# Attention in steps of a large and a small query block, with whole chunks of filling between them

## The chip, the core and the metric

The kernel runs on one core of one Trainium2 chip. The metric is the device time of one launch in microseconds (us), as the median of several runs. The core has a matrix engine (TensorE, in the profile PE for the matmuls and PEld for its weight loads), VectorE (DVE), ScalarE (ACT), GpSimd (POOL) and SyncE (SP), which issues almost all DMAs. Matmul results lie in PSUM, which has eight banks of 128 partitions x 512 fp32 values; PE writes them, DVE and ACT read them out.

## What is computed

One layer of a streaming encoder: 1,024 frames of a new stream (prompt) and 32 next frames of a running one (sample), 1,024 channels, 16 heads of 64. The part that matters here is the attention of a head, causal, with a bias from cumulated forget gates:

```
s = jnp.einsum('bqhd,bkhd->bhqk', q.astype(jnp.float32), k.astype(jnp.float32))
bias = jnp.transpose(cq, (0, 2, 1))[:, :, :, None] - jnp.transpose(ck, (0, 2, 1))[:, :, None, :]
mask = qpos[:, None] >= kpos[None, :]
s = jnp.where(mask[None, None], s + bias, jnp.finfo(jnp.float32).min)
p = jax.nn.softmax(s, axis=-1)
o = jnp.einsum('bhqk,bkhd->bqhd', p, v.astype(jnp.float32))
```

A query block is 128 frames, so block i (0 to 7) of a head has 128 (i + 1) keys. Beside the attention stand ten projections of the normed input, a depthwise convolution of 31 taps with a LayerNorm, and three output projections.

## The kernel before

All projections are three matmuls per product (high and low parts of both operands, L104), in chunks of 352 columns: a chunk is 8 x 3 matmuls into one bank, and three chunks and one weight (load, cast on ACT L93, subtraction on POOL L96) make one of 8 tiles of a gate. The kernel has three parts: projections with the convolution's taps on DVE, the attention stage, and the output projections.

The attention stage is filled up: between its own work PE does the projections of the gates gb, ma and mb, whose results nobody needs until later. `filler()` hands out 22 tiles (66 chunks), `fill(n)` runs the next n eighths of a chunk (3 matmuls each), and ScalarE copies each finished chunk out (L755) for a store to DRAM. Also hidden in this stage are the last convolution channel's taps on DVE (L260) and the LayerNorm's sums (`layernorm()`, PE L993), advanced by `next(ln)`.

A block of a head goes through three calls:

- `scores()`: 2 matmuls (L917, L918) for up to 512 keys, else 2 x 2 in two banks; then on DVE the diagonal's mask (L920) and the row maximum (L922), on ACT the exp (L925), on DVE a reciprocal (L927), on POOL the division (L928). Blocks 0 to 3 are small (bank tag S1, one bank), 4 to 7 large (tag S, two banks). Each tag has one buffer, so a score waits until the exp before has read it.
- `turn()`: P is transposed on PE (L938), up to four 128x128 pieces per bank of the pool psT, and copied by ACT (first bank) and DVE (second bank) to the tile pt of its half of the head (L941).
- `values()`: once per half of a head (blocks 0 to 3 small, 4 to 7 large), when its four blocks are turned: pt times V (L952) in column tiles of 64, copied by ACT (L957) and added by DVE (L958).

Blocks follow in the order 4, 0, 5, 1, 6, 2, 7, 3, with scores four blocks ahead. The main loop does per block: scores of the block four ahead, turn of this one, `fill(4)` (12 matmuls), then, if the block before ended a half, its values. So the large half's values come behind block 3's turn and filling, the small half's a block later. Four samples of the running stream (`Sample`: 4 heads each, scores L861 and L862, turn L883 and L886, values L898) are put into the list after head 3, 7, 11 and 15's first block; their scores use the score banks of tag S.

PE's instructions stand in the order of the program; the orders of DVE, ACT, POOL and SP are a scheduler's.

PSUM in this stage: one bank pq and one pq2 in turn for the fillings, three for psS (S and S1), three for psT.

Of the kernel before, what the change touches and what calls it, by code (L numbers as in the profile page):

```python
# [8 lines left out]
F32 = mybir.dt.float32  # L9
# [7 lines left out]
T = 1024  # L17
TS = 32
TT = T + TS
PAST = 512  # L20
# [10 lines left out]
NFILL = 22  # L31
R_U, R_V, R_QK, R_G, R_A = 0.25, 0.17, 0.19, 0.27, 0.12
NWARM = 46
ORDER = (4, 0, 5, 1, 6, 2, 7, 3)
AHEAD = 4
SAT = (2, 6, 10, 14)
SKEYS = PAST + TS
VC = 260
# [12 lines left out]
def build(tc, xT, xt, wv, wf, ckT, cv, clT, stT, vec, cst, yT, kT, vO, lfO, cpT, csT):  # L51
    nc = tc.nc
    es = ExitStack()
    PS = bass.MemoryType.PSUM

    def pool(name, bufs=1, stack=es, **kw):
        return stack.enter_context(tc.tile_pool(name=name, bufs=bufs, reuse_waits="tile", **kw))
# [88 lines left out]
    def steps(key, rh, rl, pspool, evac):  # L146

        w = split.pop(key) if key in split else split_w(load_raw(key))
        for c in range(3):
            ps = pspool.tile([128, CH], F32, name="pj", tag="pj")  # L150
            for kt in range(KT):
                mms(ps, w, rh, rl, csl(c), range(kt, kt + 1), kt == 0, kt == KT - 1)
                beat()
                if (c, kt) == (0, 5) and not split:
                    fetch()
                if kt < KT - 1:
                    yield False
            with tc.high_priority(offset=4000):
                evac(c, csl(c), ps)
            yield True  # L160
# [13 lines left out]
    def t352(name, bufs):  # L174
        return sg.tile([128, CH], F32, name=name, tag=name, bufs=bufs)

    pq = pool("pq", 1, space=PS)
# [3 lines left out]
    class Banks:  # L181

        n = 0

        def tile(self, *a, **k):
            self.n += 1
            return (pq if self.n % 5 == 4 else pjA).tile(*a, **k)
# [172 lines left out]
    ks_t = cp.tile([128, 8, TS], F32, name="ks_t")  # L360
    os_t = cp.tile([128, 8, TS], F32, name="os_t")
    rs9 = cp.tile([128, 9], F32, name="rs9")
    cq = cp.tile([128, 4], F32, name="cq")
# [10 lines left out]
    rows = lambda t: min(128, TT - 128 * t)  # L374
# [138 lines left out]
    p2 = ExitStack()  # L513
# [49 lines left out]
    for c in range(4):  # L563
# [13 lines left out]
        for t in range(8):  # L577
            ps = pj.tile([128, 512], F32, name="pjv", tag="pj")
            n = 0
# [169 lines left out]
    def gate_steps(g, f, pj):  # L749
        def ev(c, sl, ps):  # L750
            t = t352("t", 3)
            if g == "ga":
                sides["silu"] = nc.scalar.activation(t, ps, AF.Silu)
            else:
                nc.scalar.copy(t, ps)  # L755
            nc.sync.dma_start(s_g[g][f, :, sl], t)

        return steps((g, f), X, XL, pj, ev)
# [30 lines left out]
    heads = [Head(h) for h in range(H)]  # L789
# [19 lines left out]
    cvt[0] = pool("cv7", 1, stack=p2, side="right")  # L809
    taps.extend(last + sums(7))  # L810
    psS = pool("psS", 1, stack=p2, space=PS)
    psT = pool("psT", 3, stack=p2, space=PS)
    pq2 = pool("pq2", 1, stack=p2, space=PS)

    class Banks2:

        n = 0

        def tile(self, *a, **k):
            self.n += 1  # L820
            return (pq, pq2)[self.n % 2].tile(*a, **k)

    pF = Banks2()
    ap = pool("ap", 2, stack=p2, side="right")

    fills = [("gb", f) for f in range(8)] + [(g, f) for g in ("ma", "mb") for f in range(8)]

    def filler():

        for n in range(NFILL):  # L830
            yield from gate_steps(*fills.pop(0), pF)

    flow = filler()

    def fill(n):
        for _ in range(n):
            next(flow, None)

    class Sample:
# [14 lines left out]

        def scores(self):
            g, kc, pf = self.g, self.kc, self.pf
            ps = psS.tile([128, 2, 512], F32, name="psS", tag="S")
            for j in range(4):
                rows = slice(64 * (j % 2), 64 * (j % 2) + 64)
                q = qs_t[rows, 2 * g + j // 2, :]  # L860
                nc.tensor.matmul(ps[32 * j:32 * j + 32, 0, :], q, kc[rows, j // 2, :], start=True, stop=True)  # L861
                nc.tensor.matmul(ps[32 * j:32 * j + 32, 1, :TS], q, ks_t[rows, 2 * g + j // 2, :],  # L862
                                 start=True, stop=True)
            nc.vector.scalar_tensor_tensor(pf[:, :PAST], ps[:, 0, :], cq[:, g:g + 1], pf[:, :PAST],
                                           op0=ALU.add, op1=ALU.subtract)
            nc.vector.scalar_tensor_tensor(pf[:, PAST:], ps[:, 1, :TS], cq[:, g:g + 1], pf[:, PAST:],
                                           op0=ALU.add, op1=ALU.subtract)
            nc.vector.tensor_add(pf[:, PAST:], pf[:, PAST:], smask)
            nm = ap.tile([128, 3], F32, name="nm", tag="nm", bufs=6)
            nc.vector.tensor_reduce(nm[:, 0:1], pf, axis=AX.X, op=ALU.max, negate=True)  # L870
            nc.scalar.activation(pf, pf, AF.Exp, bias=nm[:, 0:1], accum_out=nm[:, 1:2])
            nc.vector.reciprocal(nm[:, 2:3], nm[:, 1:2])
            nc.vector.tensor_scalar(pf, pf, nm[:, 2:3], None, op0=ALU.mult)
# [94 lines left out]
    for n, pt_ in enumerate(PT):  # L968
        for j in range(4 * n, 4 * n + 4, 2):
            nc.gpsimd.memset(pt_[:, j + 1, 128 * (j % 4):128 * (j % 4) + 128], 0.0)  # L970
    seq = []
    for h in heads:
        seq += [Block(h, i) for i in ORDER]
        if h.h - 1 in SAT:
            seq.insert(len(seq) - 7, Sample(SAT.index(h.h - 1)))

    def first(b):
        return getattr(b, "i", None) == ORDER[0]

    def start(b):  # L980
        if first(b):
            h = b.head
            if h.h % 2 == 0:
                h.ot = heads[h.h + 1].ot = ap.tile([128, T], F32, name="ot", tag="ot", bufs=2)
        b.scores()

    def pending(b):
        return isinstance(b, Sample) or b.i % 4 == 3

    def over_channels(acc, put):  # L990
        for c in range(3):
# [5 lines left out]
    def layernorm():  # L997

        shift = sides["shift"]
        for _ in range(4):  # L1000
            yield
        yield from over_channels(mean, lambda sl, ps: nc.scalar.mul(mean[:, sl], ps, 1.0 / D))

        def put(sl, ps):
            t = t352("t", 3)
            nc.scalar.activation(t, mean[:, sl], AF.Square)
            nc.vector.scalar_tensor_tensor(rstd[:, sl], ps, 1.0 / D, t, op0=ALU.mult, op1=ALU.subtract)  # L1007
            nc.vector.tensor_add(mean[:, sl], mean[:, sl], shift[:, sl])
            nc.vector.tensor_scalar(rstd[:, sl], rstd[:, sl], EPS, None, op0=ALU.add)

        yield from over_channels(rstd, put)
        for c in range(6):
            sl = slice(c * CH // 2, c * CH // 2 + CH // 2)
            v, y = rstd[:, sl], t352("t", 3)[:, :CH // 2]
            nc.scalar.activation(y, v, AF.Ln)
            nc.scalar.activation(y, y, AF.Exp, scale=-0.5)
            yield
            w = t352("t", 3)[:, :CH // 2]
            nc.vector.tensor_copy(w, v)
            newton(v, w, y)  # L1020
            yield
# [3 lines left out]
    ln = layernorm()  # L1025
    sides["shift"] = ap.tile([128, TT], F32, name="shift", bufs=1)
    nc.sync.dma_start(sides["shift"], s_m)
    start(seq[0])
    fill(8)
    for b in seq[1:AHEAD]:  # L1030
        start(b)
        fill(2)
    for n, b in enumerate(seq):
        if n + AHEAD < len(seq):
            start(seq[n + AHEAD])
        if n + AHEAD + 2 < len(seq) and first(seq[n + AHEAD + 2]):
            seq[n + AHEAD + 2].head.load()
        if n + AHEAD + 3 < len(seq) and isinstance(seq[n + AHEAD + 3], Sample):
            seq[n + AHEAD + 3].load()
        if isinstance(b, Sample):  # L1040
            fill(4)
            b.turn()
        else:
            b.turn()
            fill(4 if b.i > 2 or b.head.h != 8 else 0)
        if n >= 1 and pending(seq[n - 1]):
            seq[n - 1].values()
        if "ready" in sides:
            next(ln, None)
    seq[-1].values()  # L1050
    for _ in flow:
        pass
    p2.close()
# [8 lines left out]
    class Banks3:  # L1062
        n = 0
# [196 lines left out]
```

## Time and profile before

| | |
|---|---|
| median of 3 runs | 1400.67 us (1399.84 to 1401.39) |
| profiled execution | 1399.91 us, of which the span of instructions 1398.1 |
| PE busy | 1383.8 us (99%) |
| DVE, ACT, POOL busy | 866.8, 602.9, 624.7 us |
| attention stage | 601.1 to 1090.1 us of the span |

The profile is of one execution. In a timeline, a row has the start and the duration in us, then engine, line of the code, operation, output<-inputs, shape and how many equal instructions are merged; in brackets the idle time of the engine just before and what ended it. [...] A list of waits has, per engine and line, what was waited for, the total in us, the number and the longest.

### The profile page before, as it was taken

To read this page: it belongs to the slowest core of one execution; us is meant where nothing else is said; L and a number is where in the kernel's file an instruction comes from. 1 tells how busy PE (TensorE), PEld (TensorE's weight loads), DVE (VectorE), ACT (ScalarE), POOL (GpSimd) and SP (SyncE) were. 2 spreads that over 40 slices of the span, in tenths; PEclk is the share of its full clock that TensorE was granted. 3 is DMA by queue.
4 is the path that set the end of the run, shared out by engine and by line. 5 is a ranking of instruction groups with operands and counts; after the bars stand their busy time and mean duration, and the time that the engine had idled before them with its cause. 6 is when DMAs were issued, how large, how long until landed. Compare 5 with 4: busy or idle time off the path is not lost.

```text
span 1398.1 us, 23429 instructions
## 1 busy us (share of the span) xinstructions
PE 1383.8 (99%) x8999; PEld 1300.6 (93%) x8999; DVE 866.8 (62%) x1199; ACT 602.9 (43%) x1180; POOL 624.7 (45%) x541
## 2 busy tenths in 40 slices
PE   8999999999999999999999999999999999999999
PEld 7999999999999999998788888888888999999998
DVE  6687787888898998646656655644443497132111
ACT  6322334656464642245444545554554555222100
POOL 2324244657585875444443533332332366254320
PEclk9999999999999999999999999999999999999999
DMA  4243332424342375334545545454542778444431
GB/s 181 93 142 92 119 109 95 150 77 158 95 164 87 121 210 153 114 104 130 144 114 159 144 140 158 121 144 115 163 115 72 280 259 268 140 143 142 147 108 47
DMA packets 102288, 192.77 MB, mean 138 GB/s; under 512 B 17248, under 2 KB 70368, under 8 KB 102176
## 3 DMA queue, kind: packets, MB, share of 16 engines
q1 hardware_dynamic: 102032, 191.21, 44.4%
q8 instruction: 71, 1.16, 0.4%
q14 instruction: 41, 0.34, 0.1%
q10 hardware_dynamic: 144, 0.07, 0.0%
HBM read 125.58 MB, written 65.64 MB: 137 GB/s over the span
## 4 chain that ended last, share of the span: by engine, by line
PE 90%; DVE 3%; issue 3%; ACT 2%; DMA 1%; POOL 1%; SPq 0%; ACTq 0%; POOLq 0%; DVEq 0%
PE pj L104 66%; PE pjv L584 7%; PE po L952 5%; PE ptr L938 4%; PE psS L917 3%; PE psS L918 2%; POOL wl L96 1%; PE pst L700 1%; PE pst L699 1%; PE po L898 0%; DVE nm L922 0%; ACT P L925 0%; DVE y L1095 0%; PE ptx L429 0%; DMA xtok<-xt 0%
## 5 line engine op out<-in xcount | busy, mean ns | idle before, releaser
L104 PE MATMUL pj<-xh,wh 128*128 128x352 f32 (+2 forms) x1536 | 508.6, 331 | 0.1
L104 PE MATMUL pj<-xl,wh 128*128 128x352 f32 (+2 forms) x1536 | 494.7, 322 | 0.2 <-DVE xl L432 0.2
L104 PE MATMUL pj<-xh,wl 128*128 128x352 f32 (+2 forms) x1536 | 493.3, 321 | 0.6 <-POOL wl L96 0.6
L96 POOL TENSOR_TENSOR wl<-raw,wh 128x384 fp32r<-128x384 f32 (+1 forms) x258 | 320.8, 1271 | 277.3 <-ACT wh L93 238.5
L260 DVE SCALAR_TENSOR_TENSOR y<-u,vec_t,y 128x1086 f32<-128x1086 f32 x240 | 382.0, 1592 | 23.4 <-ACT y L257 19.3
L104 PEld LDWEIGHTS pj<-xh,wh 128*128 128x128 f32 x1536 | 288.6, 188 | 3.2 <-issue 1.2
L104 PEld LDWEIGHTS pj<-xh,wl 128*128 128x128 f32 x1536 | 289.3, 188 | 1.1 <-POOL wl L96 0.9
L104 PEld LDWEIGHTS pj<-xl,wh 128*128 128x128 f32 x1536 | 288.5, 188 | 1.4 <-DVE xl L432 1.2
L928 POOL TENSOR_SCALAR P<-P,nm 128x640 f32<-128x640 f32 (+7 forms) x128 | 117.4, 918 | 257.0 <-DVE nm L927 244.6
L93 ACT CAST wh<-raw 128x1024 fp32r<-128x1024 f32 x86 | 90.1, 1047 | 111.0 <-PE pj L104 80.3
L925 ACT ACTIVATE P<-psS,nm 128x640 f32<-128x640 f32 (+7 forms) x128 | 95.2, 744 | 58.1 <-DVE nm L922 54.3
L941 ACT COPY pt<-ptr 128x512 f32<-128x512 f32 (+3 forms) x128 | 64.7, 506 | 96.2 <-PE ptr L938 95.0
L922 DVE TENSOR_REDUCE nm<-psS 128x1 f32<-128x640 f32 (+7 forms) x128 | 96.5, 755 | 7.9 <-POOL P L928 0.5
L717 POOL TENSOR_TENSOR ql<-qn,qh 128x352 fp32r<-128x352 f32 (+1 forms) x48 | 65.4, 1363 | 68.4 <-ACT qh L716 55.0
L920 DVE TENSOR_TENSOR psS<-psS,cmask 128x128 f32<-128x128 f32 x128 | 38.0, 297 | 78.6 <-PE psS L918 78.1
L938 PE MATMUL ptr<-ident,P 128*128 128x128 f32 x576 | 84.6, 273 | 0.3 <-DVE rstd L1007 0.3
L952 PE MATMUL po<-pt,V 128*64 128x512 f32 (+1 forms) x384 | 75.6, 529 | 0.0
L938 PEld LDWEIGHTS ptr<-ident,P 128*128 128x128 f32 x576 | 68.5, 140 | 6.6 <-DVE rstd L1007 0.5
L584 PE MATMUL pjv<-vwh,xh 128*128 128x260 f32 x256 | 72.5, 283 | 0.0
L584 PE MATMUL pjv<-vwl,xh 128*128 128x260 f32 x256 | 72.4, 283 | 0.0
L584 PE MATMUL pjv<-vwh,xl 128*128 128x260 f32 x256 | 72.3, 282 | 0.0
L917 PE MATMUL psS<-KB,QB 128*128 128x384 f32 (+1 forms) x192 | 70.1, 366 | 2.0 <-ACT P L925 1.4
(200 smaller groups left out, 2239.8 us busy)
## 6 DMA issues: line engine op xcount, KB each, us to landing
raw<-wf SPq DMA_DIRECT2D x88, 512.0 KB
QB<-s_q SPq DMA_DIRECT2D x32, 256.0 KB
KB<-s_k SPq DMA_DIRECT2D x32, 256.0 KB
kT<-qn SPq DMA_DIRECT2D x8, 528.0 KB
s_ga<-t SPq DMA_DIRECT2D x24, 176.0 KB
s_gb<-t SPq DMA_DIRECT2D x24, 176.0 KB
s_ma<-t SPq DMA_DIRECT2D x24, 176.0 KB
s_mb<-t SPq DMA_DIRECT2D x24, 176.0 KB
```

What stands on the lines that cost most here:

```text
L93: nc.scalar.copy(wh, raw)
L96: nc.gpsimd.tensor_sub(wl[:, k0:k1, :], raw[:, k0:k1, :], f32(wh[:, k0:k1, :]))
L104: nc.tensor.matmul(ps, a[:, kt, :], b(kt, sl), start=(first and n == 0), stop=(last and n == N - 1))
L260: t = nc.vector.scalar_tensor_tensor(y, u[:, i:i + CW], w, y, op0=ALU.mult, op1=ALU.add)
L584: nc.tensor.matmul(ps[:, :VC], a, b, start=(n == 0), stop=(n == 23))
L717: nc.gpsimd.tensor_sub(ql[:, :n], qn[:, o], f32(qh[:, :n]))
L917: nc.tensor.matmul(ps[:, b, :w], QB[:, qsl], KB[:, ksl], start=True, stop=False)
L922: nc.vector.tensor_reduce(nm[:, 0:1], ps[:, :nb, :w], axis=AX.XY, op=ALU.max, negate=True)
L925: nc.scalar.activation(P[:, :nk].rearrange("p (b w) -> p b w", b=nb), ps[:, :nb, :w], AF.Exp, bias=nm[:, 0:1], accum_out=nm[:, 1:2])
L928: nc.gpsimd.tensor_scalar(P[:, :nk], P[:, :nk], nm[:, 2:3], 1.0, op0=ALU.mult, op1=ALU.mult)
L938: nc.tensor.transpose(pt[:, 128 * j:128 * j + 128], P[:, 128 * (4 * u + j):128 * (4 * u + j) + 128], ident)
L952: nc.tensor.matmul(po[64 * o:64 * o + 64, q0:], V[:, j + o, hd], p[:, j + o, q0:], start=(j == 0), stop=(j == njb - 2), skip_group_check=True)
```

## The change

The list of blocks becomes a list of 64 steps, each with a large block (4 + j) and a small one (j) of the same head. A step does the scores of both blocks of the step two ahead, at a head's start (every fourth step) the two values of the head before, one behind the other, then both turns, and then `fill(8)`, one whole chunk. Fillings have one bank (pq), psT has four; the samples' scores use two banks of psT, and their three calls stand in consecutive steps. Loads of heads stand three steps ahead of a head's first turn, those of samples three steps ahead of their scores. `next(ln)` runs twice per step. One chunk of filling is left for the end, behind the last values.

```diff
-ORDER = (4, 0, 5, 1, 6, 2, 7, 3)
-AHEAD = 4
...
-    psT = pool("psT", 3, stack=p2, space=PS)
-    pq2 = pool("pq2", 1, stack=p2, space=PS)
...
+    psT = pool("psT", 4, stack=p2, space=PS)
...
-            yield from gate_steps(*fills.pop(0), pF)
+            yield from gate_steps(*fills.pop(0), pq)
...
-            ps = psS.tile([128, 2, 512], F32, name="psS", tag="S")
+            ps = [psT.tile([128, 512], F32, name="psR", tag="T") for _ in range(2)]
...
+    seq = [(Block(h, 4 + j), Block(h, j)) for h in heads for j in range(4)]
...
+    sample = {4 * h + 5: Sample(g) for g, h in enumerate(SAT)}
...
-    start(seq[0])
+    start(0)
     fill(8)
-    for b in seq[1:AHEAD]:
-        start(b)
-        fill(2)
-    for n, b in enumerate(seq):
-        if n + AHEAD < len(seq):
-            start(seq[n + AHEAD])
...
-            fill(4 if b.i > 2 or b.head.h != 8 else 0)
-        if n >= 1 and pending(seq[n - 1]):
-            seq[n - 1].values()
+    start(1)
+    heads[1].load()
+    for k in range(NS):
+        start(k + 2)
+        if k + 5 < NS and k % 4 == 3:
+            seq[k + 5][0].head.load()
+        if k + 3 in sample:
+            sample[k + 3].load()
+        if k % 4 == 0 and k:
+            for b in seq[k - 1]:
+                b.values()
+        if k - 2 in sample:
+            sample[k - 2].values()
+        if k in sample:
+            sample[k].scores()
+        for b in seq[k]:
             b.turn()
+        if k - 1 in sample:
+            sample[k - 1].turn()
+        fill(8)
         if "ready" in sides:
             next(ln, None)
-    seq[-1].values()
+            next(ln, None)
+    for b in seq[-1]:
+        b.values()
```

What the built programs have on PE at the end of the first head, before: the values of its large half stand alone between a filling and the next scores (po is the values' bank, psS the scores', ptr2 the turns', pj the fillings').

```order
L104 MATMUL pj_6793<-xl_87,wh_6653 128x352
L952 MATMUL po_6829<-pt2_6440,V_6121 64x512 x6
L952 MATMUL po_6829<-pt2_6440,V_6121 64x256 x2
L917 MATMUL psS_6840<-KB_6623,QB_6621 128x448
L918 MATMUL psS_6840<-KA_6622,QA_6620 128x448
L917 MATMUL psS_6840<-KB_6623,QB_6621 128x448
L918 MATMUL psS_6840<-KA_6622,QA_6620 128x448
L938 MATMUL ptr2_6852<-ident_189,P_6701 128x128 x4
```

The small half's values follow 12 filling matmuls later. The same place on PE after, from the small block's scores on:

```order
L904 MATMUL psS_6832<-KB_6525,QB_6523 128x384
L905 MATMUL psS_6832<-KA_6524,QA_6522 128x384
L939 MATMUL po_6842<-pt2_6437,V_6121 64x512 x6
L939 MATMUL po_6842<-pt2_6437,V_6121 64x256 x2
L939 MATMUL po_6853<-pt1_6436,V_6121 64x512 x2
L939 MATMUL po_6853<-pt1_6436,V_6121 64x256 x2
L925 MATMUL ptr2_6860<-ident_189,P_6670 128x128 x4
L925 MATMUL ptr2_6866<-ident_189,P_6670 128x128
L925 MATMUL ptr2_6869<-ident_189,P_6680 128x128
L102 MATMUL pj_6872<-xh_86,wh_6702 128x352
```

Both halves' values now stand together, between scores and turns, and three turning banks are asked for right behind them.

The start of the stage on PE, before: ahead of the scores of block 6 (448 columns per bank) stand those of block 1 and six filling matmuls.

```order
L917 MATMUL psS_6529<-KB_6112,QB_6110 128x256
L918 MATMUL psS_6529<-KA_6111,QA_6109 128x256
L104 MATMUL pj_6503<-xh_86,wh_6343 128x352
L104 MATMUL pj_6503<-xh_86,wl_6345 128x352
L104 MATMUL pj_6503<-xl_87,wh_6343 128x352
L104 MATMUL pj_6503<-xh_86,wh_6343 128x352
L104 MATMUL pj_6503<-xh_86,wl_6345 128x352
L104 MATMUL pj_6503<-xl_87,wh_6343 128x352
L917 MATMUL psS_6545<-KB_6112,QB_6110 128x448
```

After, from the scores of block 5 on:

```order
L904 MATMUL psS_6500<-KB_6112,QB_6110 128x384
L905 MATMUL psS_6500<-KA_6111,QA_6109 128x384
L904 MATMUL psS_6500<-KB_6112,QB_6110 128x384
L905 MATMUL psS_6500<-KA_6111,QA_6109 128x384
L904 MATMUL psS_6512<-KB_6112,QB_6110 128x256
L905 MATMUL psS_6512<-KA_6111,QA_6109 128x256
L904 MATMUL psS_6534<-KB_6112,QB_6110 128x448
```

No filling is left between the scores of blocks 5 and 6, which use the same two banks.

DVE at the first sample's scores (pf is the sample's row tile), before: the sample's scores are read in two operations (the rows of pf), and the reads of a block's scores lie before and after.

```order
L920 TENSOR_TENSOR psS_7314<-psS_7314,cmask_191 128x128
L941 COPY pt2_6440<-ptr2_7332 128x3x128
L922 TENSOR_REDUCE nm_7320<-psS_7314 128x1
L927 RECIPROCAL nm_7320<-nm_7320 128x1
L864 SCALAR_TENSOR_TENSOR pf_7256<-psS_7361,cq_198,pf_7256 128x512
L866 SCALAR_TENSOR_TENSOR pf_7256<-psS_7361,cq_198,pf_7256 128x32
```

After, DVE in the first sample's step:

```order
L907 TENSOR_TENSOR psS_7530<-psS_7530,cmask_191 128x128
L909 TENSOR_REDUCE nm_7536<-psS_7530 128x1
L907 TENSOR_TENSOR psS_7542<-psS_7542,cmask_191 128x128
L851 SCALAR_TENSOR_TENSOR pf_7308<-psR_7552,cq_198,pf_7308 128x512
L853 SCALAR_TENSOR_TENSOR pf_7308<-psR_7553,cq_198,pf_7308 128x32
L909 TENSOR_REDUCE nm_7546<-psS_7542 128x1
```

The sample's scores are now read behind the large block's mask and reduction and the small block's mask, and from two banks of psT.

More of the change, by code (lines that the diff above doesn't have):

```diff
@@ L811, in build @@
     psS = pool("psS", 1, stack=p2, space=PS)
-    psT = pool("psT", 3, stack=p2, space=PS)
-    pq2 = pool("pq2", 1, stack=p2, space=PS)
[L815 to L823, printed above, removed]
+    psT = pool("psT", 4, stack=p2, space=PS)
     ap = pool("ap", 2, stack=p2, side="right")
@@ L860, in scores @@
                 q = qs_t[rows, 2 * g + j // 2, :]
-                nc.tensor.matmul(ps[32 * j:32 * j + 32, 0, :], q, kc[rows, j // 2, :], start=True, stop=True)
-                nc.tensor.matmul(ps[32 * j:32 * j + 32, 1, :TS], q, ks_t[rows, 2 * g + j // 2, :],
+                nc.tensor.matmul(ps[0][32 * j:32 * j + 32, :], q, kc[rows, j // 2, :], start=True, stop=True)
+                nc.tensor.matmul(ps[1][32 * j:32 * j + 32, :TS], q, ks_t[rows, 2 * g + j // 2, :],
                                  start=True, stop=True)
-            nc.vector.scalar_tensor_tensor(pf[:, :PAST], ps[:, 0, :], cq[:, g:g + 1], pf[:, :PAST],
+            nc.vector.scalar_tensor_tensor(pf[:, :PAST], ps[0], cq[:, g:g + 1], pf[:, :PAST],
                                            op0=ALU.add, op1=ALU.subtract)
-            nc.vector.scalar_tensor_tensor(pf[:, PAST:], ps[:, 1, :TS], cq[:, g:g + 1], pf[:, PAST:],
+            nc.vector.scalar_tensor_tensor(pf[:, PAST:], ps[1][:, :TS], cq[:, g:g + 1], pf[:, PAST:],
                                            op0=ALU.add, op1=ALU.subtract)
@@ L970, in build, with start @@
             nc.gpsimd.memset(pt_[:, j + 1, 128 * (j % 4):128 * (j % 4) + 128], 0.0)
[L971 to L983, printed above, removed]
+    seq = [(Block(h, 4 + j), Block(h, j)) for h in heads for j in range(4)]
+    NS = len(seq)
+    def start(k):
+        if k < NS:
+            h = seq[k][0].head
+            if k % 8 == 0:
                 h.ot = heads[h.h + 1].ot = ap.tile([128, T], F32, name="ot", tag="ot", bufs=2)
-        b.scores()
-    def pending(b):
-        return isinstance(b, Sample) or b.i % 4 == 3
+            for b in seq[k]:
+                b.scores()
+    sample = {4 * h + 5: Sample(g) for g, h in enumerate(SAT)}
     def over_channels(acc, put):
@@ L1027, in build @@
     nc.sync.dma_start(sides["shift"], s_m)
-    start(seq[0])
+    start(0)
     fill(8)
-    for b in seq[1:AHEAD]:
-        start(b)
-        fill(2)
-    for n, b in enumerate(seq):
-        if n + AHEAD < len(seq):
-            start(seq[n + AHEAD])
[L1036 to L1041, printed above, removed]
-            b.turn()
-        else:
-            b.turn()
-            fill(4 if b.i > 2 or b.head.h != 8 else 0)
-        if n >= 1 and pending(seq[n - 1]):
-            seq[n - 1].values()
+    start(1)
[13 more added lines that the diff above has]
+            sample[k].scores()
+        for b in seq[k]:
+            b.turn()
+        if k - 1 in sample:
+            sample[k - 1].turn()
+        fill(8)
         if "ready" in sides:
             next(ln, None)
-    seq[-1].values()
+            next(ln, None)
+    for b in seq[-1]:
+        b.values()
     for _ in flow:
```

## The prediction

> **What bounds the kernel now.** I read the page first: which engine is full, and over what.
>
> ```profile
> PE 1383.8 (99%) x8999; PEld 1300.6 (93%) x8999; DVE 866.8 (62%) x1199; ACT 602.9 (43%) x1180; POOL 624.7 (45%) x541
> ```
>
> TensorE (PE) is full. The change touches only the attention stage, so next I asked for the busy times of that stage alone (from 601.1 us, the first scores, to 1090.1, the last values) and for PE's waits in it.
>
> ```profile
> 601.10:1090.10 489.00, 484.39 (x3187) 413.00 (x3185) 268.55 (x588) 244.53 (x540) 181.72 (x196) 1.00 0.46 129
> ```
>
> ```profile
> PE psS L861 <- ACT P L925: 2.3, 2, 1.3
> PE psS L917 <- ACT P L925: 1.4, 1, 1.4
> PE psS L917 <- ACT t L753: 0.6, 1, 0.6
> PE ptr L938 <- DVE rstd L1007: 0.3, 1, 0.3
> ```
>
> The columns of the first are the stretch, its length, then PE, PEld, DVE, ACT, POOL busy, clock, DMA share, GB/s. PE lacks 4.6 us of 489, and the four rows of waits (total, times, longest) name all of it: two of the four sample scores, one score at the start, the first score (banks of the old pools), one turn behind the LayerNorm. The granted clock is 1.00. So no more than 4.6 us can come from waits; anything else must come from PE's own time, and a busy PE here is not PE at its peak. That shows only in the starts of neighbouring matmuls. First PE's timeline at a head's end:
>
> ```profile
> 1025.45 0.32 PE L104 MATMUL pj<-xl,wh 128*128 128x352 f32 x1
> 1025.71 3.23 PE L952 MATMUL po<-pt,V 128*64 128x512 f32 x16
> 1028.87 0.47 PE L917 MATMUL psS<-KB,QB 128*128 128x448 f32 x1
> 1029.18 0.37 PE L918 MATMUL psS<-KA,QA 68*128 68x448 f32 x1
> 1029.39 0.37 PE L917 MATMUL psS<-KB,QB 128*128 128x448 f32 x1
> ...
> 1029.80 0.71 PE L938 MATMUL ptr<-ident,P 128*128 128x128 f32 x5
> 1030.26 0.41 PE L104 MATMUL pj<-xh,wh 128*128 128x352 f32 x1
> ...
> 1032.35 1.51 PE L952 MATMUL po<-pt,V 128*64 128x512 f32 x8
> 1033.79 0.44 PE L917 MATMUL psS<-KB,QB 128*128 128x384 f32 x1
> ```
>
> The large half of a head's values (x16) takes 3.16 us from its start to the next start, the small half (x8) 1.44. Around them PE loses time without an idle entry: the filling matmul ahead takes 0.26 to the next start, and the score behind 0.31 where the next of its kind takes 0.21. What a filling matmul takes in peace, and what the two halves take one behind the other, is seen at the end of the stage, where the last head's halves already stand so:
>
> ```profile
> 1085.73 4.52 PE L952 MATMUL po<-pt,V 128*64 128x512 f32 x24
> 1090.18 0.43 PE L104 MATMUL pj<-xh,wh 128*128 128x352 f32 x1
> 1090.44 0.32 PE L104 MATMUL pj<-xh,wl 128*128 128x352 f32 x1
> 1090.60 0.32 PE L104 MATMUL pj<-xl,wh 128*128 128x352 f32 x1
> ```
>
> That is 4.45 us for both, then 0.26 for the first filling matmul and 0.16 for the next.
>
> **Term 1, the values.** Apart, a head's halves cost 3.16 + 1.44 and, twice, 0.10 of entry (0.26 - 0.16) and 0.10 behind (0.31 - 0.21): 5.00. Together they cost 4.45 + 0.10 + 0.10 = 4.65. The changed order puts them together for the 15 heads that had them apart: 15 x 0.35 = 5.2 us less. [...] What the trace doesn't show is the new neighbourhood: scores ahead and transposes behind. From below the pair spares only the entry of the second half, 15 x 0.10 = 1.5; from above, both edges cost as shown and the turn restarts at no loss, 15 x 0.40 = 6.0. I take 5.2, since the quoted pair is the same code.
>
> **Term 2, merging scores, turns and fillings.** The matmuls stay the same in number: 64 steps of 24 filling matmuls replace 128 of 12, and of the 22 fillings' chunks one is now left behind the last values. A turn's edge costs nothing worth a term: five transposes take 0.46 to the next start (1029.80 to 1030.26), which is 0.09 each, as if the filling hid one. Taken at 0, bounds -1 and +1 us (64 edges at 0.016 either way).
>
> **Term 3, the start.** Now the second score waits longer.
>
> ```profile
> 610.14 1.28 DVE L922 TENSOR_REDUCE nm<-psS 128x1 f32<-128x768 f32 x2
> ...
> 610.54 0.32 PE L104 MATMUL pj<-xl,wh 128*128 128x352 f32 x1
> 611.18 0.90 ACT L925 ACTIVATE P<-psS,nm 128x768 f32<-128x768 f32 x1 [3.05 <-DVE nm L922]
> ...
> 612.23 0.47 PE L917 MATMUL psS<-KB,QB 128*128 128x448 f32 x1 [1.37 <-ACT P L925]
> ```
>
> ```profile
> 1037.42 0.30 DVE L920 TENSOR_TENSOR psS<-psS,cmask 128x128 f32<-128x128 f32 x1 [0.39 <-PE psS L918]
> 1037.83 1.23 DVE L922 TENSOR_REDUCE nm<-psS 128x1 f32<-128x1024 f32 x1
> ```
>
> Block 6 needs the two banks of block 5, free when its exp is done. Before, 12 filling matmuls and block 1's scores lay between them and PE still lost 1.69 - 0.16 = 1.53 us (610.54 to 612.23). After, only block 1's two score matmuls of 256 columns lie there (0.24, by the 0.21 that one of 448 takes). From the end of the large scores: 0.2 until DVE starts, two masks at 0.30, the reduction of 768 columns at about 0.95 (an estimate: 1.23 for 1,024, less a quarter, plus a fixed part), exp 0.90, and 0.15 from exp's end (612.08) to PE: 2.8, less 0.24: 2.5 us. So +1.0; if a convolution tap stands ahead on DVE up to +2.4, if the masks overlap +0.5.
>
> **Term 4, the samples.** They leave the double score bank for two of the four turning banks.
>
> ```profile
> 686.10 1.09 PE L861 MATMUL psS<-kc,qs_t 64*32 64x512 f32 x8 [1.31 <-ACT P L925]
> ...
> 687.18 0.55 PE L938 MATMUL ptr<-ident,P 128*128 128x128 f32 x3
> ```
>
> ```profile
> 687.37 0.75 DVE L864 SCALAR_TENSOR_TENSOR pf<-psS,cq,pf 128x512 f32<-128x512 f32 x1 [1.12 <-DMA QA<-s_q]
> ```
>
> The waits of 2.3 us go. What is late next: a sample's step asks for five turning banks, and the fifth, the small block's turn, waits until DVE has read the sample's scores. DVE has ahead of that read the large mask, the large reduction and the small mask. From the end of the large scores: 0.2, 0.30, 1.23 with 0.1 between, 0.30, 0.75, less overlaps of 0.2: 2.7. PE gets there at 0.46 (small scores, two matmuls of 512 at the rate of the 0.21 for 448) + 1.08 (686.10 to 687.18) + 6 x 0.11 for the large turn = 2.2. Loss 0.5 in each of four samples: 2.0. A step later the sample's own turn takes two more banks, the second of them that of the large turn; its copy stands on ACT behind the filling's copy and, at the first and the last sample, behind a weight cast:
>
> ```profile
> L755 ACT COPY t<-pj 128x352 f32<-128x352 f32 x66 | 29.7, 451 | 23.9 <-PE pj L104 20.5 <-issue 1.6 <-DMA QB<-s_q 0.7
> ...
> L93 ACT CAST wh<-raw 128x1024 fp32r<-128x1024 f32 x22 | 23.2, 1053 | 0.0
> ```
>
> 0.45 + 1.05 from the step's start, and the copy itself: about 0.2 lost at the first (with scores ahead) and 0.7 at the last (none). In all 2.9 for 2.3: +0.6, bounds -2.3 (all hidden) and +2.
>
> **Term 5, the LayerNorm sums.** Two per step, in two turning banks; one small turn then waits behind a cast and two ACT copies, about 0.7 us where 0.3 was lost: +0.4, bounds -0.3 and +1.
>
> **Hidden edits.** Loads of heads and samples are issued one to two steps earlier; no DMA is in the list of PE's waits, so this gains nothing; SP only holds them earlier. The small turn behind a head's values needs the bank of the large half. ACT copies, then DVE adds:
>
> ```profile
> 1028.98 0.58 ACT L957 COPY ot<-po 64x512 f32<-64x512 f32 x1 [3.85 <-PE po L952]
> ...
> 1029.59 0.69 DVE L958 TENSOR_TENSOR ot<-ot,po 64x512 f32<-64x512 f32 x1 [4.27 <-ACT ot L957]
> ```
>
> The bank is free 1.4 us after the large half ends (1028.87 to 1030.28). PE covers it with the small half, 1.4, and five or six transposes, 0.5: 0.5 us to spare.
>
> **The sum.** -5.2 + 0 + 1.0 + 0.6 + 0.4 = -3.2. The profiled execution took 1399.91 us (span 1398.1, 1.8 around it), 0.76 below the runs' median of 1400.67; 1400.67 - 3.2 = 1397.5 us.
>
> **The rivals.**
> *No change (0.30).* The switch spares less, since the transposes behind the values lose what the scores lost, or the start and samples take their upper bounds. Half of term 1 (2.6) against +2.0 of waits gives -0.6: 1400. For it: the three terms of waits are chains of queued work, whose errors are mostly upward. Against: the pair at 1085.73 shows the gain itself.
> *The bank at the head's end (0.12), slower.* If ACT and DVE are later than the 0.5 us to spare when the large half ends, the small turn waits, and PE with it, at 15 heads. A cast of 1.05 just ahead of the copy would cost 1.05 - 0.5 = 0.55 each time: 15 x 0.55 = 8.3, less 3.2, is +5: 1405.7. It decides from 0.7 us of lateness on (3.2 / 15 past the cover). For it: a cast does stand ahead of the copy at every third step. Against it: ACT had waited 3.85 us for PE ahead of the copy at 1028.98, and the built order puts the step's exps behind these copies.
> *One bank for the fillings (0.08), slower.* Each chunk now waits for the copy of the chunk before: 0.45 us plus 0.2, or with a cast first 1.7, against 1.8 us of scores and turns. It decides where ACT is over a microsecond late; one step in four losing 0.6 gives 16 x 0.6 - 3.2 = +6.4: 1407. [...]
>
> **How the numbers follow.** The forecast, 0.50, is the sum as it stands or better. About 0.2%, 2.8 us, is what a measurement of this kernel can tell from no change, so the forecast lies just beyond it, and a small miss in the waits moves it to the next case. Faster 0.50, same 0.30, slower 0.20 (0.12 + 0.08). The range reaches down to term 1 at 6.0 with half of the new waits hidden, -3.2 - 0.8 - 3.0 = -7: 1393.7; up, past the case of no change, to the milder half of the slower cases, 1404.
>
> **What would show it.** In the profile after: 16 groups of values x24 of about 4.45 us each, in place of 32; PE's waits led by a score at the stage's start (2.3 to 2.5) and a turn behind DVE in the four sample steps; no wait of a turn on the values' addition at heads' ends, none of a filling on its copy. The stage, with its last chunk of 3.8 us, shorter by 3 us. I am wrong if the turn behind the values starts slowly, or if PE's waits pass 8 us.

## The result, and the profile after

| | before | changed |
|---|---|---|
| median of 6 runs, us | 1400.74 (1399.84 to 1401.91) | 1393.47 (1392.55 to 1396.22) |
| ratio | | 0.9949 (95%: 0.9936 to 0.9962) |
| profiled execution: time, span, us | 1399.91, 1398.1 | 1396.22, 1394.4 |
| of its span: ahead of the first attention score | 602.07 | 605.62 |
| attention stage, to the end of the 66th chunk of filling | 488.11 | 482.54 |
| behind it | 307.92 | 306.24 |

The change took off 7.3 us; the forecast was 3.2 us, and the measured time lies 0.2 us below its range. The profiled execution of the changed kernel is the slowest of its six, and the split of its span says where: it has 3.5 us more ahead of the attention stage, in which PE does the same matmuls in the same order in both kernels. (A wait for a weight there is 1.4 us longer, 1.99 for 0.58, and two stretches of 3.41 us at a granted clock of 0.50 lie there, from 19.89 and from 593.33; see the last section.) The stage itself is 5.6 us shorter and what lies behind it 1.7 us. Those two add up to the 7.3, but one execution of each kernel can't show that the other runs split the same way: the stage of a second profile, below, is only 4.1 shorter. The table counts the stage from the start of the first score at 602.07, not from 601.1 as the prediction did.

The stage in the changed kernel, as the windows give it (the 66th chunk, which now runs behind the last values, is counted in), and PE's waits in it:

```profile
605.62:1088.16 482.54, 478.90 (x3185) 416.69 (x3185) 260.16 (x591) 237.73 (x539) 165.47 (x196) 1.00 0.46 131
```

```profile
PE psS L904 <- ACT P L912: 2.3, 1, 2.3
PE ptr L925 <- DVE pf L851: 1.3, 4, 0.3
PE psS L904 <- ACT t L751: 0.6, 1, 0.6
```

The waits are those forecast, in number and length: one score at the start, the small turn in four sample steps, and the old first score. They add up to 4.2 us where before had 4.6, so nearly all of what the stage lost, it lost inside PE's busy time. A head's end of the changed kernel on PE's timeline, where rows overlap (a filling matmul in peace lasts 0.32 and the next starts 0.16 after it, at 1084.50 and 1084.66), so that what a matmul costs is read from start to start:

```profile
994.12 4.52 PE L939 MATMUL po<-pt,V 128*64 128x512 f32 x24
```

```profile
1021.80 0.34 PE L904 MATMUL psS<-KB,QB 128*128 128x384 f32 x1
1021.98 0.33 PE L905 MATMUL psS<-KA,QA 68*128 68x384 f32 x1
1022.24 4.52 PE L939 MATMUL po<-pt,V 128*64 128x512 f32 x24
1026.69 0.87 PE L925 MATMUL ptr<-ident,P 128*128 128x128 f32 x6
1027.32 0.41 PE L102 MATMUL pj<-xh,wh 128*128 128x352 f32 x1
```

The pair takes 4.45 from start to start, as the last head's did before. The score ahead of it takes 0.26 where the one before it takes 0.18, and six transposes behind it 0.63 where six took 0.58 before (the median of 16): entry 0.08, exit 0.05. From pair to pair a head without sample takes 28.12 here (994.12 to 1022.24).

Behind the stage, PE's waits of before and of the changed kernel:

```profile
PE pj L104 <- POOL wl L96: 1.5, 3, 0.7
```

```profile
PE pj L102 <- POOL wl L94: 0.6, 1, 0.6
```

The prediction never looked there. Before, PE waits for a weight's low part at 1172.47 (0.52), 1174.46 (0.27) and 1197.59 (0.70); in the changed kernel the first is still there (0.58) and the other two are gone.

### The profile page after: what moved, and what is told of

It is laid out like the page before. It is cut to its first block, busy times and chain, and to the rows that moved or that the text cites. A ratio compares the mean times of both kernels' runs of the same rounds, so it can differ in the third digit from the quotient of the medians.

```text
span 1394.4 us, 23413 instructions
## 1 busy us (share of the span) xinstructions
PE 1380.5 (99%) x8999; PEld 1307.9 (94%) x8999; DVE 853.1 (61%) x1199; ACT 597.1 (43%) x1180; POOL 610.1 (44%) x541
## 3 DMA queue, kind: packets, MB, share of 16 engines
q8 instruction: 71, 1.16, 0.4%
## 4 chain that ended last, share of the span: by engine, by line
PE 93%; DVE 2%; issue 2%; POOL 1%; ACT 1%; DMA 0%; POOLq 0%; ACTq 0%; DVEq 0%
PE pj L102 68%; PE pjv L582 7%; PE po L939 5%; PE ptr L925 5%; PE psS L905 3%; PE psS L904 2%; POOL wl L94 1%; PE warm L345 1%; PE pst L698 1%; PE ptx L427 1%; PE pst L697 1%; PE po L885 0%; DVE y L1079 0%; POOL c_l L1088 0%; DVE y L1083 0%
## 5 line engine op out<-in xcount | busy, mean ns | idle before, releaser
L94 POOL TENSOR_TENSOR wl<-raw,wh 128x384 fp32r<-128x384 f32 (+1 forms) x258 | 326.0, 1291 | 282.7 <-ACT wh L91 241.7
L915 POOL TENSOR_SCALAR P<-P,nm 128x640 f32<-128x640 f32 (+7 forms) x128 | 96.1, 763 | 259.6 <-DVE nm L914 259.3
L909 DVE TENSOR_REDUCE nm<-psS 128x1 f32<-128x640 f32 (+7 forms) x128 | 92.4, 750 | 1.9 <-DVE psS L907 0.2
L753 ACT COPY t<-pj 128x352 f32<-128x352 f32 x72 | 32.5, 452 | 117.1 <-PE pj L102 112.9
L925 PE MATMUL ptr<-ident,P 128*128 128x128 f32 x576 | 76.3, 277 | 1.3 <-DVE pf L851 1.3
L925 PEld LDWEIGHTS ptr<-ident,P 128*128 128x128 f32 x576 | 63.9, 141 | 10.0 <-issue 7.9
L939 PE MATMUL po<-pt,V 128*64 128x512 f32 (+1 forms) x384 | 72.3, 525 | 0.0
```

The lines of the kernel that those rows point to most:

```text
L94: nc.gpsimd.tensor_sub(wl[:, k0:k1, :], raw[:, k0:k1, :], f32(wh[:, k0:k1, :]))
L909: nc.vector.tensor_reduce(nm[:, 0:1], ps[:, :nb, :w], axis=AX.XY, op=ALU.max, negate=True)
L915: nc.gpsimd.tensor_scalar(P[:, :nk], P[:, :nk], nm[:, 2:3], 1.0, op0=ALU.mult, op1=ALU.mult)
L925: nc.tensor.transpose(pt[:, 128 * j:128 * j + 128], P[:, 128 * (4 * u + j):128 * (4 * u + j) + 128], ident)
L939: nc.tensor.matmul(po[64 * o:64 * o + 64, q0:], V[:, j + o, hd], p[:, j + o, q0:], start=(j == 0), stop=(j == njb - 2), skip_group_check=True)
```

## The experiments

Each kernel was timed against the kernel before on the same chip and profiled once. "Stage" and "behind" are the stretches of the table above. The expectations from the second group on (from the chunk at the start) count the stage to the last full-width matmul of values, 0.53 us shorter for every kernel and "rest" as much longer; the table uses the longer count. "Behind" is what is left of a span printed to 0.1 us, so it is good to 0.05.

| kernel | ratio to before (95%) | first score | stage | behind |
|---|---|---|---|---|
| before, second profile | one run | 603.34 | 488.12 | 307.84 |
| changed, second profile | 0.9949 (0.9937 to 0.9960) | 603.80 | 484.03 | 306.28 |
| halves apart again | 0.9980 (0.9971 to 0.9988) | 603.87 | 487.54 | 306.09 |
| before, halves together | 0.9955 (0.9943 to 0.9967) | 603.39 | 482.25 | 307.66 |
| fillings split | 0.9945 (0.9933 to 0.9956) | 605.11 | 479.66 | 306.32 |
| chunk at the start | 0.9945 (0.9933 to 0.9956) | 605.15 | 479.94 | 307.71 |
| the same, chunk left behind | 0.9940 (0.9928 to 0.9952) | 603.01 | 480.64 | 306.15 |
| sample's scores late | 0.9950 (0.9938 to 0.9963) | 604.77 | 481.90 | 306.83 |
| combined | 0.9911 (0.9898 to 0.9923) | 603.61 | 477.47 | 306.12 |
| start 7 and 1 | 0.9934 (0.9921 to 0.9948) | 603.77 | 480.64 | 306.09 |
| start 4 and 4, fillings split | 0.9930 (0.9918 to 0.9942) | 603.58 | 479.65 | 306.07 |
| the same, scores split | 0.9922 (0.9909 to 0.9935) | 602.24 | 479.54 | 306.42 |

**The two kernels again.** No edit.

> The changed kernel once more, unchanged, for a second profile. The first profiled execution took 1396.22 us where the other five took 1392.55 to 1393.79; its records show 3.5 us more ahead of the attention stage than before (first score at 605.6 against 602.1), with one wait of 2.0 us on a weight's low part and ten slow matmuls behind it. If that is of this execution alone: median 1393.5, first score within 0.5 of 602, attention stage 482.5 us (before 488.1), and behind the stage again 1.6 us less than before, with one wait of about 0.7 on a weight. If it is of the kernel: first score at 605 again. If the 1.6 us behind the stage is chance: three or four waits on weights there, 2.2 us, as before.

> The kernel before, unchanged, for a second profile. Its first profile had its first score at 602.1, behind one wait of 0.74 us on a weight at 589; every other kernel here waited 1.7 to 2.1 us there and began at 603 to 605.6. If that wait is of the execution or the chip: about 1.8 now, first score at 603 to 605. If it is of the order: 0.74 and 602.1 again. The stage 487.6 and the rest 308.4 again in either case.

The changed kernel's median was 1394.37, and behind the stage it was again 1.6 us shorter, so that part is the kernel's. The stretch ahead is of the execution: the second profile of before waited 1.61 us for the weight at 589 (0.58 in the first). By the starts, that is from one matmul's start to the next less the 0.16 that it takes in peace, they cost 1.77 and 0.74. Its first score stands at 603.34, within the 602.2 to 605.6 of all other kernels. The stage of before came out the same within 0.01 us; that of the changed kernel 1.5 us longer than in its first profile, all of it at the start (below, on the clock).

**Halves apart in the new order.**

```
-        if k % 4 == 0 and k:
-            for b in seq[k - 1]:
-                b.values()
...
-        for b in seq[k]:
+        for j, b in enumerate(seq[k]):
+            if k % 4 == 0 and k:
+                seq[k - 1][j].values()
             b.turn()
```

> The changed order with a head's two halves of values apart again: the large half, the large turn of the next step, the small half, the small turn. Theory A (the pair carries the gain): each of 15 heads pays another entry, another exit and the slower halves, 0.35 to 0.44 us, so 5.2 to 6.6 us: 1399 to 1400, attention stage 488 to 489. Theory B (merged scores, turns and fillings carry it, and the pair spares only the 0.15 between 3.16 + 1.44 and 4.45): 15 x 0.15 = 2.3, 1395.8, stage 484.8.

**Halves together in the old order.**

```
-        if n >= 1 and pending(seq[n - 1]):
+        if n >= 1 and isinstance(seq[n - 1], Sample):
             seq[n - 1].values()
+        if getattr(b, "i", None) == 3:
+            seq[n - 1].values()
+            b.values()
...
-    seq[-1].values()
```

> The order of before, block by block, with only the values of a head's two halves put one behind the other. Theory A: 5.2 to 6.6 us less than before: 1394.1 to 1395.5, stage 481.5 to 483, with 16 groups of 24 values at 4.45 each. Theory B: 2.3 us less: 1398.4, stage 485.8. Behind the stage as before (2.2 us of waits on weights), since no chunk of filling is left behind the last values.

Values on PE's timeline: first the pairs of two heads in the old order, then one head's halves, apart, in the new order:

```profile
993.52 4.52 PE L952 MATMUL po<-pt,V 128*64 128x512 f32 x24
...
1021.83 4.52 PE L952 MATMUL po<-pt,V 128*64 128x512 f32 x24
1026.28 0.47 PE L917 MATMUL psS<-KB,QB 128*128 128x448 f32 x1
```

```profile
1024.82 3.23 PE L939 MATMUL po<-pt,V 128*64 128x512 f32 x16
1027.98 0.76 PE L925 MATMUL ptr<-ident,P 128*128 128x128 f32 x5
1028.68 1.51 PE L939 MATMUL po<-pt,V 128*64 128x512 f32 x8
1030.12 0.33 PE L925 MATMUL ptr<-ident,P 128*128 128x128 f32 x1
```

Over the six heads without sample or LayerNorm sums, from large half to large half, the mean is 28.61 us before, 28.26 in the old order with the pair, 28.16 in the changed kernel and 28.49 with the halves apart again. Pairing takes off 0.35 a head from the old order, and parting puts 0.33 a head back on the new one: 5.2 and 5.0 us over 15 heads, from both sides. Theory A holds and theory B falls. In the old order the stage lost 5.9 us in all; the 0.7 beyond the 5.2 is in the two heads with the LayerNorm sums, where the row of PE waiting for rstd (0.5 by the starts) is gone too.

**Turns and fillings split.**

```
-        for b in seq[k]:
-            b.turn()
+        seq[k][0].turn()
+        fill(4)
+        seq[k][1].turn()
         if k - 1 in sample:
             sample[k - 1].turn()
-        fill(8)
+        fill(4)
```

> The changed order with turns and fillings split again: the large turn, half a chunk, the small turn, half a chunk. Scores and values stay merged. Theory A: a turn's edge gives back what a filling's edge costs (0.085 hidden in each turn, 0.08 in each filling's first matmul), so 64 more of each cost 0 within 1 us: 1393.5, stage 482.5; the four waits of a sample's step (0.49 each, 2.0) may go, since half a chunk now stands ahead of the small turn: down to 480.5. Theory B: 64 x 0.05 to 0.1 = 3 to 6 us more: 1397 to 1400, stage 485.5 to 488.5.

The plain steps kept their length to 0.02 us each: for this kernel, merging turns and fillings is worth nothing, as theory A has it. Each sample's step went from 7.84 to 7.33, 4 x 0.5 = 2.0, and PE's waits in the stage have no row for pf:

```profile
PE psS L904 <- ACT P L912: 2.3, 1, 2.3
PE psS L904 <- ACT t L751: 0.6, 1, 0.6
PE pj L102 <- ACT t L753: 0.2, 1, 0.2
```

Its stage is 2.9 shorter, 0.9 more than the samples give: 1.5 from a start without a dip of the clock (below), less 0.5 at a filling that waits for its copy in the second sample's head (0.2 in the list; the head, which should have lost 0.5 as the other three did, is as long as in the changed kernel, 32.17 and 32.20).

**A chunk at the start, and with one left behind.** The first adds the first line, the second both changes.

```
     heads[1].load()
+    fill(8)
     for k in range(NS):
...
-        fill(8)
+        fill(8 if k != 62 else 0)
```

> The changed order with one whole chunk of filling put between the start's second pair of scores and the first step of the loop, so that none is left behind the last values. Inside the stage the wait of 2.3 us of the third pair of scores goes: stage 479.7 us for 482.0. Theory C (what lies behind the stage hangs on the chunk that is left behind the last values, since ScalarE's built order there goes back to that of before): the rest of the program 308.3 us again for 306.8, with 2.2 us of waits on weights, so in all 0.7 less than the changed kernel: 1392.8. Theory D (the 1.6 us behind the stage come from the shorter stage or from chance): rest 306.8, 1391.2.

> The same chunk at the start, and the last step but one goes without its filling, so that again one chunk is left behind the last values. Stage 479.7, plus at most 0.6 for the last turn, which loses the cover of a chunk. Theory C: ScalarE's order behind the stage is that of the changed kernel, rest 306.8: 1391.2 to 1391.8. Theory D: no difference from the kernel with the chunk at the start alone but the cost of the last turn.

The row of the score waiting for exp is gone in both. Behind the stage the first is back at 307.71 and the second at 306.15, with these waits there, first and second kernel:

```profile
PE pj L102 <- POOL wl L94: 1.3, 3, 0.5
```

```profile
PE pj L102 <- POOL wl L94: 0.6, 1, 0.6
```

Theory C holds. In all 14 profiles, the four of kernels that leave no chunk behind the last values have 307.7 to 307.9 behind the stage, the ten others 306.1 to 306.8. PE's matmuls there are the same; what differs is the order of work on ScalarE, and on VectorE and GpSimd too, and each group has one order in common. ScalarE at the casts of the two weights that PE waits for, in the kernel before, then in the changed one:

```profile
1168.99 1.27 ACT L1096 ACTIVATE y<-y,vec_t 128x1056 f32<-128x1056 f32 x1 [2.40 <-DVE y L1095]
1170.16 1.03 ACT L93 CAST wh<-raw 128x1024 fp32r<-128x1024 f32 x1
...
1194.96 0.50 ACT L1138 ACTIVATE sma<-sma 128x352 f32<-128x352 f32 x1 [1.46 <-DMA sma<-s_ma]
1195.37 1.04 ACT L93 CAST wh<-raw 128x1024 fp32r<-128x1024 f32 x1
```

```profile
1164.74 1.08 ACT L1087 CAST c_h<-y 128x1056 fp32r<-128x1056 f32 x1 [1.26 <-DVE y L1083]
1165.72 1.04 ACT L91 CAST wh<-raw 128x1024 fp32r<-128x1024 f32 x1
1166.67 1.27 ACT L1081 ACTIVATE y<-y,vec_t 128x1056 f32<-128x1056 f32 x1
...
1188.26 0.50 ACT L1123 ACTIVATE sma<-sma 128x352 f32<-128x352 f32 x1 [4.23 <-DMA sma<-s_ma]
1188.66 1.04 ACT L91 CAST wh<-raw 128x1024 fp32r<-128x1024 f32 x1
```

Before, the first cast stands behind an activation that waits 2.40 us for VectorE, and GpSimd's low parts, made from the cast, reach PE late (it waits to 1172.47); in the changed kernel the cast stands ahead of that activation. PE's first wait is no shorter for it, since GpSimd now does another low part first (to 1168.37), but its later ones for this weight are gone: by the starts 0.7 us. The second cast gives more, 1.0: before, it ends at 1196.41 and PE waits to 1197.59; in the changed kernel it ends at 1189.70, and PE gets to the same matmul at 1193.84 without a wait. That the order on ScalarE alone does it is read from these rows, not tried; nor was why the scheduler turns the orders around when a chunk is left behind the last values.

The first kernel came out at the changed kernel's time (1393.50; by the ratio 0.6 less, which its interval does not tell from 0.7 less or from nothing), though its stage is 2.6 shorter in the profile. The second took 1392.3, 0.5 above theory C's range. Part of what the start gave was lost again at the second sample, whose own turn now waits 1.16 us for its softmax (first kernel; 1.17 in the second):

```profile
830.49 1.28 PE L925 MATMUL ptr<-ident,P 128*128 128x128 f32 x10
832.93 0.66 PE L870 MATMUL ptr<-ident,pf 128*128 128x128 f32 x4 [1.16 <-DVE pf L860]
```

**The sample's scores behind the turns.**

```
-        if k in sample:
-            sample[k].scores()
         for b in seq[k]:
             b.turn()
+        if k in sample:
+            sample[k].scores()
```

> The changed order with a sample's scores behind the step's two turns in place of ahead of them. Theory A (the small turn's bank waits until VectorE has read the sample's scores behind mask, reduction and mask): the four waits go, 4 x 0.49 = 2.0 us less: 1391.5, stage 480.0, no row of PE waiting for pf at the turn. Rival: the wait moves to the sample's own turn a step later, whose softmax then starts 1.4 us later, or to the bank of the large turn: 0 to 1 us less.

The wait's row is gone, but a sample's step went from 7.84 only to 7.69: 0.15, so 0.6 in all. The rival had the size, and neither had the reason. The sample's scores in the changed kernel, and then in this one:

```profile
707.14 1.08 PE L848 MATMUL psR<-kc,qs_t 64*32 64x512 f32 x8
708.02 0.26 PE L849 MATMUL psR<-ks_t,qs_t 64*32 64x32 f32 x8
708.21 0.88 PE L925 MATMUL ptr<-ident,P 128*128 128x128 f32 x6
709.41 0.41 PE L925 MATMUL ptr<-ident,P 128*128 128x128 f32 x2 [0.33 <-DVE pf L851]
```

```profile
707.22 1.39 PE L848 MATMUL psR<-kc,qs_t 64*32 64x512 f32 x8
708.10 0.57 PE L849 MATMUL psR<-ks_t,qs_t 64*32 64x32 f32 x8
708.60 0.43 PE L102 MATMUL pj<-xh,wh 128*128 128x352 f32 x1
```

The sixteen matmuls of 64 x 32 take 1.38 to the next start behind turns and 1.07 behind scores: 0.31 of the 0.49 is paid again at these edges, with no idle entry.

**What the runs pointed to, combined.** The chunk at the start and the split fillings, with the last two steps at half a filling.

```
     heads[1].load()
+    fill(8)
...
+        seq[k][0].turn()
+        fill(4)
+        seq[k][1].turn()
...
-        fill(8)
+        fill(4 if k < 62 else 0)
```

> What the runs point to, together: the changed order with turns and fillings split (large turn, half a chunk, small turn, half a chunk), one chunk at the start, and the last two steps with half of their filling, so that one chunk is left behind the last values. If the parts add: stage 482.0 - 2.9 - 2.3 = 476.8, rest 306.8: 5.2 less than the changed kernel, 1388.3. If the last steps wait without their cover, up to 1 us more.

1388.6, as expected: 12 us below before and the fastest of all. What is left of PE's waits in its stage:

```profile
PE psS L904 <- ACT t L751: 0.6, 1, 0.6
PE po L885 <- ACT pts L871: 0.6, 1, 0.6
```

**One eighth of the start's filling moved.**

```
     start(0)
-    fill(8)
+    fill(7)
     start(1)
+    fill(1)
```

> The changed order with one eighth of the first chunk of filling moved from ahead of the start's second pair of scores to behind it, so that the third pair's wait falls from 2.33 to 1.85 us. Theory E (a wait of more than about 2 us is followed by some 4 us at a granted clock of 0.5 to 0.8, which cost the changed kernel another 1.65 us at the start, 613.8 to 617.2): the clock stays at 1.00 there, stage 482.0 - 0.5 - 1.65 = 479.9, in all 1391.4. Theory F (the clock's dip has nothing to do with the wait's length): 0.5 less, stage 481.5.

The score waited 1.99 us, 0.34 less than 2.33, and the stage was 1.9 shorter. The third pair of scores in the changed kernel and here:

```profile
613.82 0.74 PE L904 MATMUL psS<-KB,QB 128*128 128x448 f32 x1 [2.33 <-ACT P L912]
614.36 0.57 PE L905 MATMUL psS<-KA,QA 68*128 68x448 f32 x1
614.74 0.57 PE L904 MATMUL psS<-KB,QB 128*128 128x448 f32 x1
```

```profile
611.67 0.47 PE L904 MATMUL psS<-KB,QB 128*128 128x448 f32 x1 [1.99 <-ACT P L912]
611.98 0.37 PE L905 MATMUL psS<-KA,QA 68*128 68x448 f32 x1
612.18 0.36 PE L904 MATMUL psS<-KB,QB 128*128 128x448 f32 x1
```

Behind the wait of 2.33 the same matmul takes 0.38 to the next start where it takes 0.20. The dip is gone, as theory E has it. But the kernel with split fillings had no dip behind its 2.33 either, and the 1.99 here falls across two stretches of the clock's grid (last section), so this run doesn't show that the shorter wait was the reason. The times don't tell either: 0.9934 within 0.0013, where E gives 0.9933 and F 0.9945.

**The start halved; scores split too.** The first has fill(4) ahead of and behind start(1) and the split fillings. The second also moves the small block's scores (at the start they keep their places):

```
-            for b in seq[k]:
-                b.scores()
+            seq[k][0].scores()
...
         seq[k][0].turn()
         fill(4)
+        if k + 2 < NS:
+            seq[k + 2][1].scores()
         seq[k][1].turn()
```

> The changed order with turns and fillings split (large turn, half a chunk, small turn, half a chunk) and the start's filling split into halves ahead of and behind the second pair of scores: nothing else is moved, and one chunk stays behind the last values. The third pair's wait falls from 2.33 to 0.4 us and no dip of the clock follows: stage 479.1 - 1.9 = 477.2 from the kernel with split fillings alone (its profile showed no dip at the start), rest 306.8: 1387.5 to 1389, as the combined kernel with a chunk at the start or a little less.

> The kernel with split fillings and a split start, and the scores split too: the small block's scores stand between the half chunk and the small turn, so that of the merging only the pair of values is left. The pieces of the earlier runs leave 2.3 us for merged scores (the stage of before less pair, waits and split fillings), so stage 2.3 longer than with merged scores, 1390. If merged scores are worth nothing, as the prediction had it, no difference.

The first missed its stage by 2 us: half a chunk covers less than was taken off, the score still waited 1.5, another 0.2 ahead of it, and a filling 0.5 for its copy. The second refutes the 2.3 us: its stage is as long as with merged scores (479.54 and 479.65). That is in part a coincidence, since it lacks the filling's wait and the last head is 0.35 longer. Its plain heads take 28.18 to 28.23, against 28.14 to 28.24 with merged scores, but for one of 28.53, in which a turn of eight transposes takes 1.07 where it takes 0.79. Merged scores are worth at most 0.05 a head beside that one. The 2.3 may have been left over from adding stages of which one had a dip of the clock and the others not.

## Why the prediction was wrong, point by point

It had the sign and the leading term right, and the size wrong: 3.2 where 7.3 were measured. The step that failed is **the sum**. It was made from the attention stage alone and set what lies behind at nothing, without a reason, though three waits for a weight's low part stood in the trace of before there; that part gave 1.7. Inside the stage it put merging 1.6, the samples 1.2 and the LayerNorm sums 0.9 too high, two of these because waits that it counted did not come, and the start 1.4 too low.

- **Term 1, the pair, -5.2.** Right: 0.35 and 0.33 a head, shown from both sides. The turn behind the values, which the trace of before could not show, restarts with a loss of 0.05; the entry costs 0.08 behind scores. What PE does at such an edge no trace shows, only what it costs. The sample's scores cost 0.31 more between turns and fillings than between scores and turns (1.38 for 1.07), so in these runs the price hangs on the neighbours.
- **Term 2, merging, 0 within 1.** About right: plain heads are 0.10 shorter than with the pair alone, 1.6 us over 16 heads, a little outside the bound. Fillings and turns are worth 0.00 to 0.02 a head, scores at most 0.05. The edges of the pair with its new neighbours give 0.07 of the 0.10: 0.08 and 0.05 where the old order has 0.10 and 0.10.
- **Term 3, the start, +1.0.** The wait was sized rightly (2.33 for 1.37), but what followed it was left out: 3.41 us at a granted clock of 0.50, worth 1.5 us. It cost 2.4 in the first profile and 3.9 in the second.
- **Term 4, the samples, +0.6.** The four waits came as worked out: 0.49 each lost, 2.0. The 0.9 for the sample's own turn did not. Its second bank was taken to be that of the same step's large turn, behind a cast on ScalarE. At the last sample, the second bank's transpose starts at 1068.81, while ScalarE begins its first copy of that step at 1068.73:

```profile
1068.32 0.60 PE L870 MATMUL ptr<-ident,pf 128*128 128x128 f32 x4
1068.81 0.28 PE L873 MATMUL ptr<-ident,pf 128*32 128x128 f32 x1
```

```profile
1067.78 1.05 ACT L91 CAST wh<-raw 128x1024 fp32r<-128x1024 f32 x1
1068.73 0.97 ACT L928 COPY pt<-ptr 128x512 f32<-128x512 f32 x2
```

  So the bank did not wait for that copy, and the order of banks was another than the one counted; which bank it was, the trace doesn't name. By the starts the term is 2.0 for the 2.6 that the two waits before cost (1.48 and 1.11; the list, without the restarts, has 2.3): -0.6.
- **Term 5, the LayerNorm sums, +0.4.** What before lost to rstd (0.3 in the list, 0.5 by the starts: eight transposes take 1.29 there and 0.81 at 929.33) is gone and no wait came for it: -0.5.
- **The hidden edits** were hidden: no turn waits for the addition at a head's end, and no filling for its copy in the changed kernel. (The loads of heads stand three steps ahead of a head's first scores, five ahead of its first turn.)
- **Left out:** behind the stage -1.7, with the other order of work there.

The sum with what was measured: -5.2 - 1.6 + 2.4 - 0.6 - 0.5 - 1.7 = -7.2. That it comes so near to 7.3 is in part luck: the 1.6 is read from six heads and taken for 16, and the start is that of one profile. Of the rivals, no change fell with term 1; the bank at a head's end and the one bank for the fillings did not show in any wait. A chunk's copy takes 0.45 us (L753), and from a chunk's last matmul to the next chunk's first the changed kernel's profile has 1.78 us or more (least at 1067.07 to 1068.85): the scores and turns between two chunks covered the copy, and no wait for it is in the list. Where a chunk was split and the start shortened, a single wait of 0.5 for the copy did appear.

## What to carry to other kernels

Take the sum over the whole span: an edit in one stage can move the order that a scheduler gives the next, and the waits that stand there are part of the stake (1.7 us here). Work of another tile shape cost 0.05 to 0.10 us here at each edge of the 128x64 values, and 0.31 more at those of the sample's scores in another place, without an idle entry; so count how often it is entered, and price its edges by the neighbours that it will have. A wait that has been removed is worth its step's change of length, not its row: with the sample's scores late, a step lost a wait of 0.49 and became 0.15 shorter.

## What the runs showed of the hardware

In these runs a wait of PE of about 2 us could cost nearly as much again behind it: the one of 2.33 at the start of the stage about 1.5. In the changed kernel's first profile, the wait at 589 (1.99) and the one at 611 (2.33) are each followed by a stretch at half the clock, the second of which is (the columns are the stretch, its length, busy times, clock, DMA share and GB/s):

```profile
610.40:613.81 3.41, 1.09 (x7) 0.89 (x6) 2.50 (x6) 1.48 (x4) 1.01 (x1) 1.00 0.55 198
613.81:617.23 3.42, 3.41 (x12) 3.14 (x13) 1.80 (x5) 0.43 (x3) 1.36 (x2) 0.50 0.00 0
```

Such a dip lasts 3.41 us at a granted clock of 0.50. That one at the start of the stage cost about 1.5 us is read from the second profile: it has two there, one right behind the other, and its stage is 1.5 longer. Four of the five profiles with a wait of 2.33 at the start had a dip, none of those with 1.99 or less there.

More than the length of the wait decided in these runs. In each of the five profiles with two dips or more ahead of the kernel's end, the dips start whole multiples of 3.413 us apart: at 19.89, 593.33 and 613.81 in the first profile, which is 168 and 6 such steps. So in these profiles the dips lie on a grid of 3.413 us that does not start with a wait, and whether one followed went with how much of the wait lay in one stretch. The fifth wait of 2.33, in the kernel with split fillings, lies across two:

```profile
609.16:612.58 3.42, 1.83 (x12) 1.63 (x10) 3.24 (x5) 0.75 (x2) 1.76 (x2) 1.00 0.59 207
612.58:615.99 3.41, 2.67 (x17) 2.55 (x18) 1.82 (x5) 1.74 (x5) 1.36 (x2) 1.00 0.00 2
```

PE is idle for 1.6 us of the first and 0.7 of the second, and no dip followed; the 1.99 of the start with one eighth moved is cut into 0.6 and 1.4. The four with a dip had 1.62 to 2.33 in one stretch. At 589 the three profiles with a dip had 1.83 to 1.87 in one stretch, and the others 1.76 or less. Idle time is not the whole of it: near the start of the span, about 1.5 us idle in a stretch was followed by a dip in four profiles (in the changed kernel's first, 1.49 from 16.47 to 19.89) and by none in four others; a wait of 1.48 there in the first profile of before was not followed by one. What sets the grid, and what else decides, the runs don't show.

Dips are part of why runs of one kernel differ by 1 to 3 us: of the runs with the halves apart, the two with a mean clock of 1.000 took 1397.5 and 1397.6, the one with 0.996 took 1401.6. The length of a step that meets no wait repeats more closely: in the changed kernel's first profile, behind the first head, the four steps of a head without a sample or LayerNorm sums take 10.23 to 10.25, 6.10 to 6.16, 5.69 to 5.71 and 6.08 to 6.12 us.
